# Sums of down-projection weights: eight of eleven moved from the in-projection to the out-projection, into slots of the raw weight ring

## The chip, the cores and the metric

The kernel runs on one core of a Trainium2 chip. The metric is the device time of one execution in microseconds (us). Engines are named as in the profile: PE is TensorE (PEld its weight loads), DVE is VectorE, ACT is ScalarE, POOL is GpSimd, SP is SyncE, whose instruction queue issues nearly all DMAs of this kernel. PE's order of instructions is written out by hand; the order on the other engines, and which buffer a tile gets, is decided by a scheduler when the program is built.

## The reference

One layer of a streaming encoder, in fp32. The input has 2048 prompt rows (16 tiles of 128) and one tile of 8 x 16 sample rows, of width 1024; the feed-forward part has width 2816.

```python
qm, km, vm, om, ip, fp, qa, ka, va = split_in(x @ w_in)
hm, C1, n1, m1 = mlstm_chunkwise(qm, km, vm, logi, logf, C0, n0, m0, mchunk)   # 4 heads x 128
hm = (og * head_norm(hm, g_mlstm_norm)).reshape(B, T, M_WIDTH)
ha = swa_prompt(rope(qa), rope(ka), va, attn_sinks)                            # 8 q, 2 kv heads x 64
mix = jnp.concatenate([hm, ha], axis=-1) @ w_out
h = layer_norm(DEEPNORM_ALPHA * x + mix, ln1_g, ln1_b)
f, conv_rows = conv_ffn(h, conv_prev, w_up, w_conv, b_conv, w_down)   # (silu(g) * a) @ w_down
y = layer_norm(DEEPNORM_ALPHA * h + f, ln2_g, ln2_b)
```

## The kernel before

Every product is made of three matmuls on halves: a fp32 operand is split into a high part (rounded, by ACT) and a low part (the rest, by DVE). Three of the four large projections also use a scheme with seven products of half-size blocks instead of eight, which needs sums and differences of blocks of the weights. The kernel runs in four stages: the in-projection (to about 625 us; four blocks of token tiles, `IBLOCKS`), the out-projection (about 626 to 905 us; five blocks `OBLOCKS` of 3, 4, 4, 4 and 2 tiles), the up-projection with convolution (to about 1840 us) and the down-projection. The mLSTM and attention work of each tile ("chains") is woven between the matmuls of the two projections before it is needed.

**The sums.** The down-projection needs differences of four quadrants of its weights: for each k from 0 to 10, rows of `wdn[k]` (x) and `wdn[11 + k]` (y). `d_sums` (L841) makes them ahead of time, in three steps that its caller gives out at chosen places: step 0 allocates the two tiles `txy` and issues the two loads of 512 KB on SP (L845, L846); step 1 makes four subtractions of 128 x 512 on DVE (L851 to L854), the first two on x's result and y, the others on both; step 2 stores both tiles to the DRAM arrays `zt[0, k]` and `zt[1, k]` (L856, L857). The arrays are read from 1838 us on (L2021). In the kernel before the tiles txy use the buffers `xr1` and `xr3` of the pool `xp`, which otherwise hold inputs: x of the in-projection and the pairs `xraw` of the out-projection (L893), each split into `oh` (ACT L897) and `ol` (DVE L898).

**The in-projection** (`i_dense`) walks over items (b, g, s): block b, weight group g of five, product s of seven. Before the change it gives out the steps of one sum in each of the items with b in (2, 3) and g in (0, 1, 2, 3): eight sums. Weights arrive in a ring of seven raw buffers, `wraw` (`WR = 7`, 4 KB in each partition): `next_raw` loads a unit into a slot, `next_split` splits it into `w` (ACT L218, DVE L219), after which the slot is free. `raw_free` allows at most four units (three once `spare` is set) to be loaded and not yet split, so that some slots of the ring stand idle.

**The out-projection** (`o_block`) makes each block in two halves of 512 output columns (`hf`). A half has eight matmul groups for each token tile; `group` yields after each of them, and `steps` counts them. A half takes four units of `wo` (L462), issued through the same ring. In the last round of half 1 the group loads the input pairs of the next block (`x_pair`). The result of a tile is taken out of PSUM by DVE into `ymix` (L1613), normalised later by `norm` (L1556 to L1573, with `lsc` on POOL, L1559), and stored to `zh`. Before the change three sums are given out here, in half 0 of blocks 1, 2 and 3.

**Queues.** A DMA in SP's queue waits for its data, for its buffer to be free, and for an earlier DMA that used the same semaphore; whatever stands behind it in the queue waits too. DVE and ACT also take their instructions in order. The steps of the chains that the prediction names: `dt`, `kw`, `qk` (L1110 to L1205) feed the matmul `pnum` (L1212); `mr` (L1154 to L1160), `ms` on POOL (L1161) and `hn` (L1157, L1167) feed the transposes `pht` (L1177); `ql` and `kringl` (L219) feed the scores `psc` (L1304), evicted by L1308; `pth` (L1344) feeds `ppo` (L1349). `cw` (L1674) is a scaling of the convolution's weights, at the end of the out-projection.

Of the kernel before, what the change touches and what calls it, by code (L numbers as in the profile page):

```python
# [8 lines left out]
F32 = mybir.dt.float32  # L9
# [5 lines left out]
P = 128  # L15
D = 1024
# [21 lines left out]
WR = 7  # L38
# [16 lines left out]
NK2 = NFF // 2  # L55
# [150 lines left out]
class Prog:  # L206
# [3 lines left out]
    def pool(self, name, bufs=1, space=None, **kw):  # L210
        if space is not None:
            kw["space"] = space
        return self.tc.tile_pool(name=name, bufs=bufs, **kw)
# [374 lines left out]
    def i_dense(self):  # L588
        nc, a = self.nc, self.a
        nb = len(IBLOCKS)  # L590
        last = NG - 1

        self.next_raw()
        self.x_load(0, 2)
        for _ in range(3):
            self.next_raw()
        self.x_load(0, 4)
        self.single_raw = self.tp.tile([P, KD, P], F32, name="xsr", tag="pth", bufs=2)
        nc.sync.dma_start(self.single_raw, a["xs"])
        self.angles = {}  # L600
        self.rope_load(IBLOCKS[0][2], 2)
        self.rope_load(NPT, 1)
        self.next_split()
        self.x_steps(0, "b12")
        for _ in range(3):
            self.next_split()
        self.x_steps(0, 3)
        self.x_single(1, 2)
        self.x_load(0, 1)
        self.next_raw()  # L610
        self.x_load(0, 3)
        self.x_steps(0, 1)
        self.advance()
        self.x_steps(0, 2, "t3", 7, "t2", 6)
        self.x_single(4)
        self.x_steps(0, "t1", 5, "t4")
        self.sb, self.trans = {}, None

        passages = [{1: ["load"], 7: ["t3", 7], 6: ["t2", 6], 3: [3, "t4"], 4: ["b12", "t1"]},
                    {1: ["load"], 6: ["t3"], 7: [7, "t2"], 5: [6], 3: [3, "t4"], 4: ["b12", "t1"]}]  # L620
        sums = 0
        after = None
        for item in self.items:
            if after:

                after[0] -= 1
                if after[0] == 3:
                    self.logs_of(after[1] - 1)
                if after[0] < 0:
                    self.i_done = after[1]  # L630
                    after = None
            self.chains.hold = item[0] == "t" and item[1] > 0
            if item[0] == "t":
                _, b, ti, e = item
                if ("g", e, 3) not in self.wu:
                    self.advance()
                if b not in self.gates:
                    self.gates[b] = self.tp.tile([P, 5, 8], F32, name="gates", tag="gates", bufs=2)
                ps = self.bank([P, 512], "pg") if ti == 4 else self.ib[ti % 2 * 2]
                yield from self.i_direct(b, ti, e, ps)  # L640
                self.i_keys(b, ti, ps)
                if ti == 1:
                    if b + 1 < nb:
                        self.x_steps(b + 1, 1, 2)
                    else:
                        self.release(4)
                    after = [6, b + 1]
                elif ti == 3 and b or ti == 4:
                    self.release(4)
                    self.x_steps(b, 4)  # L650
                    if b:
                        self.x_steps(b, 5)
                self.advance()
                continue
            _, b, g, s = item
            if item not in self.wu:
                self.advance()
            yield from self.i_product(b, g, s)
            del self.wu[item]
            self.release(2)  # L660
            if self.trans and s != 4:
                self.i_transposes()
            with self.tc.high_priority():
                behind = self.i_after(b, g, s)
            if (b, g, s) == (0, 0, 7):
                self.t_setup()
            if (g, s) == (1, 6):
                self.rope_load(IBLOCKS[b][0], 2)
            if g == last and b + 1 < nb:
                if s == 7:  # L670
                    self.rope_load(IBLOCKS[b + 1][2], 2)
                for x in passages[b > 0].get(s, ()):
                    if x == "load":
                        self.spare = True
                        self.x_load(b + 1, 1, 2, 3, 4)
                    else:
                        self.x_steps(b + 1, x)
            if g == last and b + 1 == nb and s in (7, 5, 2, 3):
                self.x_pair(0, (7, 5, 2, 3).index(s))
            with self.tc.issue_after(behind) if behind and b == 0 else nullcontext():  # L680
                self.advance()

            if b >= nb // 2 and g < last:

                steps = (6, 2, 5) if g == last - 1 else (6, 5, 3)
                if s in steps:
                    self.d_sums(sums, steps.index(s))
                    sums += s == steps[2]
        self.sums = sums
        self.logs_of(nb - 1)  # L690
        self.chains.hold = False
# [146 lines left out]
                              out[:, i * HT:(i + 1) * HT].rearrange("p (f m) -> p f m", f=2))  # L838


    def d_sums(self, k, step):  # L841
        nc, V = self.nc, self.nc.vector
        if step == 0:
            self.txy = x, y = [self.xp.tile([P, D], F32, name="txy", tag=f"xr{q}", bufs=1) for q in (1, 3)]
            nc.sync.dma_start(x, self.a["wdn"][k])  # L845
            nc.sync.dma_start(y, self.a["wdn"][NK2 + k])  # L846
            return
        x, y = self.txy
        if step == 1:
            l, r = slice(0, 512), slice(512, D)  # L850
            V.tensor_sub(x[:, l], x[:, r], x[:, l])  # L851
            V.tensor_sub(x[:, r], y[:, r], x[:, r])
            V.tensor_sub(y[:, r], y[:, r], x[:, l])
            V.tensor_sub(y[:, l], y[:, l], y[:, r])  # L854
            return
        nc.sync.dma_start(self.zt[0, k], x)  # L856
        nc.sync.dma_start(self.zt[1, k], y)  # L857
# [730 lines left out]
    def o_block(self, b):  # L1588
        nc, nb = self.nc, len(OBLOCKS)
        tiles = OBLOCKS[b]  # L1590

        ys = self.ynext + [self.o_x(t) for t in tiles[len(self.ynext):]]
        self.ynext = []

        outs = [self.fp.tile([P, D], F32, name="ymix", tag="hst", bufs=2) for _ in tiles] if b == nb - 1 else ys
        for hf in range(2):
            c = slice(hf * 512, hf * 512 + 512)
            steps = 0
            for cost, ti, ps in self.group(b, tiles, 8 * b + 4 * hf, hf == 1):
                yield cost  # L1600
                if ps is None:
                    steps += 1
                    if hf and b + 1 < nb and steps == 8 * len(tiles) - 6:
                        self.ynext = [self.o_x(t) for t in OBLOCKS[b + 1][:2]]
                    if steps % 2 == 0 and self.norms and next(self.norms[0], self) is self:
                        del self.norms[0]
                    if hf == 0 and b and self.sums < NK2 and steps in (2, 14, 20):
                        self.d_sums(self.sums, (2, 14, 20).index(steps))
                        self.sums += steps == 20
                    continue  # L1610
                y = outs[ti]
                with self.tc.high_priority():
                    nc.vector.scalar_tensor_tensor(y[:, c], ys[ti][:, c], ALPHA, ps, op0=ALU.mult, op1=ALU.add)  # L1613
                if hf and b == nb - 2 and ti >= len(tiles) - 2:

                    nc.sync.dma_start(self.zh[tiles[ti]], y)
                elif hf and b < nb - 1:
                    self.norms.append(self.norm(y, *self.ln1, self.zh[tiles[ti]]))
        assert b < nb - 1 or self.sums == NK2
        self.late = list(zip(outs, tiles))  # L1620
# [575 lines left out]
```

## Time and profile before

| | us |
|---|---|
| median of 3 runs | 2308.32 |
| lowest and highest | 2305.21, 2309.71 |
| profiled execution | 2306.25 |
| its span in the trace | 2304.5 |

The profile is of one execution. The span is the time from the first to the last instruction in it; the time of the execution is 1.75 us longer. A row of a timeline gives the start, the duration, the engine, the line, the operation with its tiles (out<-in) and, in brackets, the idle time of the engine before it and what ended it. A table of windows gives for each stretch the busy time of every engine. A view of waits sums up, for one engine, the idle time by the instruction that waited and by what it waited for.

### The profile page before, as it was taken

What the parts mean: (1) busy time and instruction counts of PE and PEld (TensorE: products, weight loads), DVE (VectorE), ACT (ScalarE), POOL (GpSimd) and SP (SyncE); (2) the same over time, 40 slices, a digit from 0 to 9 for tenths busy, and PEclk for the clock granted to TensorE, in tenths of its full rate; (3) what the DMA queues carried; (4) which work ended last, traced back from release to release, by engine and by line L of the source; (5) the groups of instructions that cost most, each with busy time, mean ns of one, the idle gap of its engine ahead of it and who ended that gap; (6) DMA issues with size and microseconds to landing.
All of it is one profiled execution on the core that took longest, in us unless ns stands there. A gap on an engine that the chain in (4) does not pass through costs nothing.

```text
span 2304.5 us, 39741 instructions
## 1 busy us (share of the span) xinstructions
PE 2278.9 (99%) x14293; PEld 2094.4 (91%) x14293; DVE 1807.4 (78%) x3075; ACT 1272.4 (55%) x2377; POOL 279.4 (12%) x509
## 2 busy tenths in 40 slices
PE   8999999999999999999999999999999999999998
PEld 8999999989877778999999999999999978888876
DVE  8787587787688888998778777678766786895987
ACT  5453476776766656555656555556555544444442
POOL 0001001100011210211112101003111200200200
PEclk9999999999999999999999999999999999999999
DMA  7988999899987757888777888878998786746742
GB/s 267 319 306 297 309 322 342 310 306 341 309 286 239 242 199 277 302 328 300 277 281 272 307 304 310 306 256 289 316 299 260 248 299 213 253 170 223 253 156 83
DMA packets 300165, 632.38 MB, mean 274 GB/s; under 512 B 47868, under 2 KB 141120, under 8 KB 299968
## 3 DMA queue, kind: packets, MB, share of 16 engines
q1 hardware_dynamic: 295296, 616.14, 77.3%
q0 software_dynamic: 3520, 10.56, 1.4%
q10 hardware_dynamic: 1152, 3.15, 0.4%
q8 instruction: 113, 1.85, 0.3%
q14 instruction: 84, 0.69, 0.1%
HBM read 458.11 MB, written 171.64 MB: 273 GB/s over the span
## 4 chain that ended last, share of the span: by engine, by line
PE 81%; DVE 4%; DMA 2%; issue 1%; ACT 1%; POOL 0%; SPq 0%; DVEq 0%; ACTq 0%; POOLq 0%
PE dps L1874 19%; PE fup L1874 19%; PE dps L705 8%; PE fup L2081 6%; PE dps L2081 6%; PE fht L2081 6%; PE dps L223 3%; PE dps L224 2%; PE dps L225 2%; PE ppo L1349 1%; PE psc L1304 1%; PE ppt L1343 1%; PE dps L731 1%; PE fht L1698 1%; PE pscore L1129 1%
## 5 line engine op out<-in xcount | busy, mean ns | idle before, releaser
L1874 PE MATMUL fup<-hh,uw 128*128 128x384 f32 (+1 forms) x1848 | 478.4, 328 | 0.0
L1874 PE MATMUL dps<-hh,uw 128*128 128x384 f32 (+1 forms) x1848 | 478.0, 328 | 0.0
L1874 PEld LDWEIGHTS fup<-hh,uw 128*128 128x128 f32 x1848 | 330.5, 188 | 0.0
L1874 PEld LDWEIGHTS dps<-hh,uw 128*128 128x128 f32 x1848 | 330.3, 188 | 0.0
L1932 DVE SCALAR_TENSOR_TENSOR cc<-u,cw,cc 128x768 f32<-128x768 f32 (+1 forms) x264 | 258.2, 979 | 62.8 <-ACT cc L1930 56.1
L1874 PE MATMUL fup<-hl,uw 128*128 128x384 f32 (+1 forms) x924 | 303.2, 328 | 0.9 <-DVE hl L219 0.9
L1874 PE MATMUL dps<-hl,uw 128*128 128x384 f32 (+1 forms) x924 | 302.8, 328 | 0.0
L705 PE MATMUL dps<-w,oh 128*128 128x256 f32 x1344 | 254.2, 284 | 0.0
L218 ACT CAST uw<-wraw 128x1024 fp32r<-128x1024 f32 x126 | 123.3, 979 | 230.4 <-PE dps L2081 122.4
L219 DVE TENSOR_TENSOR w<-wraw,w 128x1024 fp32r<-128x1024 f32 (+2 forms) x167 | 189.7, 1142 | 66.0 <-ACT w L218 61.9
L218 ACT CAST w<-wraw 128x1024 fp32r<-128x1024 f32 (+2 forms) x167 | 163.0, 984 | 119.0 <-PE dps L705 61.9
L705 PEld LDWEIGHTS dps<-w,oh 128*128 128x128 f32 x1344 | 210.7, 188 | 10.8 <-issue 8.1
L219 DVE TENSOR_TENSOR uw<-wraw,uw 128x1024 fp32r<-128x1024 f32 x126 | 142.5, 1131 | 62.3 <-ACT uw L218 62.2
L705 PE MATMUL dps<-w,ol 128*128 128x256 f32 x672 | 188.1, 280 | 0.0
L1874 PEld LDWEIGHTS fup<-hl,uw 128*128 128x128 f32 x924 | 173.9, 188 | 1.7 <-DVE hl L219 1.5
L2081 PE MATMUL fup<-uw,fu 128*128 128x512 f32 x726 | 174.0, 396 | 1.2 <-ACT fht L2089 1.2
L1874 PEld LDWEIGHTS dps<-hl,uw 128*128 128x128 f32 x924 | 173.8, 188 | 0.0
L705 PE MATMUL dps<-oh,w 128*128 128x256 f32 x896 | 169.6, 285 | 3.6 <-DVE w L219 1.3
L2081 PEld LDWEIGHTS fup<-uw,fu 128*128 128x128 f32 x726 | 136.6, 188 | 34.3 <-ACT fht L2089 1.6
L2081 PE MATMUL dps<-uw,fu 128*128 128x512 f32 x660 | 165.3, 396 | 1.1 <-DVE uw L219 1.1
L1930 ACT ACTIVATE cc<-u,cw 128x768 f32<-128x768 f32 (+1 forms) x132 | 132.0, 1001 | 46.2 <-DVE u L1912 22.2
L2081 PEld LDWEIGHTS dps<-uw,fu 128*128 128x128 f32 x660 | 124.1, 188 | 31.2 <-DVE uw L219 1.5
(318 smaller groups left out, 4590.0 us busy)
## 6 DMA issues: line engine op xcount, KB each, us to landing
uw<-zw SPq DMA_DIRECT2D x176, 512.0 KB, 5.1
zw<-uw SPq DMA_DIRECT2D x88, 512.0 KB, 3.3
w<-zws SPq DMA_DIRECT2D x72, 512.0 KB, 5.8
wv<-wup SPq DMA_DIRECT2D x66, 512.0 KB, 4.4
wraw<-wi SPq DMA_DIRECT2D x65, 512.0 KB, 5.5
wraw<-zt SPq DMA_DIRECT2D x60, 512.0 KB, 4.1
wraw<-wdn SPq DMA_DIRECT2D x45, 512.0 KB, 4.5
wraw<-wo SPq DMA_DIRECT2D x40, 512.0 KB, 4.7
```

The source lines that it names most:

```text
L218: nc.scalar.copy(hi, src)
L219: return nc.vector.tensor_sub(lo, src, hi.bitcast(F32)).ins
L223: mm(out, ah, bh, start=start, stop=False)
L224: mm(out, ah, bl, start=False, stop=False)
L225: mm(out, al, bh, start=False, stop=stop)
L705: mm(o, l, r, start=s in (1, 7) and c == k == i == 0, stop=k == 3 and i == 2, skip_group_check=True)
L731: mm(o, x, w, start=k == i == 0, stop=k == KD - 1 and i == 2, skip_group_check=True)
L1129: self.nc.tensor.matmul(ps[:, h], qk[:, 4 + h], qk[:, h], start=True, stop=True)
L1874: mm(ps, l[:, k], r[:, k], start=s in (1, 7) and k == 0 and i == 0, stop=k == 3 and i == 2, skip_group_check=True)
L1930: S.activation(c[:, v], u[:, 2:2 + n], AF.Identity, bias=w[3], scale=w[2])
L1932: V.scalar_tensor_tensor(c[:, v], u[:, i:i + n], w[i], c[:, v], op0=ALU.mult, op1=ALU.add)
L2081: mm(ps, l[:, k, c], r[:, k], start=s in (1, 4, 7) and u == 0 and k == 0 and i == 0, stop=u == nu - 1 and k == n - 1 and i == 2, skip_grou ...
```

## The change

Three sums stay in the in-projection, given out at (b, g) = (2, 1), (3, 0) and (3, 2). The other eight are given out in the out-projection, one in each half of blocks 0 to 3, at the steps 2 (loads), 18 (subtractions) and 22 (stores). Those eight take their two tiles from the ring of raw weights (`ring=True`) instead of `xr1` and `xr3`. The three that stay in the in-projection use `xr1` and `xr3` as before. The number of instructions, of DMAs and of bytes, and what they compute, stay the same, and so does the order of PE's instructions.

```diff
@@ i_dense
-            if b >= nb // 2 and g < last:
-
-                steps = (6, 2, 5) if g == last - 1 else (6, 5, 3)
+            if (b, g) in ((nb - 2, 1), (nb - 1, 0), (nb - 1, 2)):
+
+                steps = (6, 5, 3)
                 if s in steps:
                     self.d_sums(sums, steps.index(s))
                     sums += s == steps[2]
@@ d_sums
-    def d_sums(self, k, step):
+    def d_sums(self, k, step, ring=False):
         nc, V = self.nc, self.nc.vector
         if step == 0:
-            self.txy = x, y = [self.xp.tile([P, D], F32, name="txy", tag=f"xr{q}", bufs=1) for q in (1, 3)]
+            pool = lambda q: (self.wp, "wraw", WR) if ring else (self.xp, f"xr{q}", 1)
+            self.txy = x, y = [p.tile([P, D], F32, name="txy", tag=tag, bufs=n) for p, tag, n in (pool(1), pool(3))]
             nc.sync.dma_start(x, self.a["wdn"][k])
             nc.sync.dma_start(y, self.a["wdn"][NK2 + k])
             return
@@ o_block
-                    if hf == 0 and b and self.sums < NK2 and steps in (2, 14, 20):
-                        self.d_sums(self.sums, (2, 14, 20).index(steps))
-                        self.sums += steps == 20
+                    if self.sums < NK2 and steps in (2, 18, 22):
+                        self.d_sums(self.sums, (2, 18, 22).index(steps), True)
+                        self.sums += steps == 22
                     continue
```

## The prediction

> **What bounds the kernel now.** I read the totals of the page first, then a table by stage, then the waits of TensorE in the two stages that the change touches, then the rows around each sum.
>
> ```profile
> span 2304.5 us, 39741 instructions
> ...
> PE 2278.9 (99%) x14293; PEld 2094.4 (91%) x14293; DVE 1807.4 (78%) x3075; ACT 1272.4 (55%) x2377; POOL 279.4 (12%) x509
> ```
>
> TensorE (PE) is busy for 2278.9 us of 2304.5, so 25.6 us are idle in the whole kernel. The change touches no matmul. It can gain no more than the idle time that hangs on the moved sums, and it loses wherever a moved sum makes TensorE wait.
>
> The table by stage has, for each stretch, its length, then busy time of PE, PEld, DVE, ACT and POOL with instruction counts, the granted clock, the DMA share and GB/s.
>
> ```profile
> core 0: us, PE busy (x) PEld busy (x) DVE busy (x) ACT busy (x) POOL busy (x), PEclk, DMA share, GB/s
> ...
> 300.00:560.00 260.00, 255.83 (x2156) 237.01 (x2154) 200.26 (x573) 185.24 (x477) 25.75 (x43) 1.00 0.94 322
> ...
> 630.00:905.00 275.00, 274.86 (x1516) 216.60 (x1515) 229.99 (x552) 170.86 (x411) 42.91 (x51) 1.00 0.73 249
> ```
>
> The stretch 300 to 560 us holds the eight sums of the in-projection: DMA is nearly full (0.94), TensorE idles 260 - 255.83 = 4.17 us. The out-projection, 630 to 905, has room on the DMA engines (0.73), but TensorE idles 0.14 us: nothing can be won there. DVE has 275 - 229.99 = 45 us free. So the most that the change can bring is 4.17 us, 0.18% of the time. Which part of it hangs on sums is told by the waits of PE from 310 to 362 and from 480 to 560 (total us, times, longest):
>
> ```profile
> PE dps L705 <- ACT mr L1154: 0.8, 1, 0.8
> PE pht L1177 <- ACT hn L1167: 0.5, 1, 0.5
> PE pnum L1212 <- issue: 0.5, 1, 0.5
> ...
> PE pnum L1212 <- issue: 1.4, 1, 1.4
> PE ppo L1349 <- ACT pth L1344: 0.6, 1, 0.6
> PE pht L1177 <- DVE ql L219: 0.2, 1, 0.2
> ```
>
> Six waits, 4.0 us together. I number the sums 0 to 10 in order of time.
>
> **Part 1: five sums leave the in-projection.** A sum is two loads of 512 KB (x, y), four subtractions on DVE, two stores. The view of the tiles txy:
>
> ```profile
> L851 DVE TENSOR_TENSOR txy<-txy x11: 667/687/693, 311.0 to 827.2; 128x512 f32<-128x512 f32 x11
> ...
>   DVE txy L852: 4.6, 3
>   DVE txy L851: 3.8, 2
> ...
> DMA to landing us min/median/max: 3.1/4.9/8.2
> ```
>
> One subtraction takes 0.687 us, so a sum is 4 x 0.687 = 2.75 us of DVE, and the five take 13.7 us of DVE and 5 x 4 x 0.5 = 10.5 MB out of the stage. On DVE five waits for loads took 4.6 + 3.8 = 8.4 us. But three sums stay, and in the order built from the changed source they stand on each queue where sums 0, 4 and 5 stood; those that go are 1, 2, 3, 6 and 7. That matters, because the longest wait of PE belongs to sum 5:
>
> ```profile
> 495.52 0.69 DVE L851 TENSOR_TENSOR txy<-txy 128x512 f32<-128x512 f32 x1 [2.91 <-DMA txy<-wdn]
> ...
> 499.55 0.69 DVE L1133 TENSOR_TENSOR dt<-pscore,dt 128x512 f32<-128x512 f32 x1
> ...
> 500.34 0.46 PE L1212 MATMUL pnum<-v,dt 128*128 128x129 f32 x2 [1.43 <-issue]
> ```
>
> DVE waited 2.91 us for x; dt stood behind it; the matmul that reads dt started 0.1 us after dt's end (499.55 + 0.69) and PE had idled 1.43. The third kept sum has the same neighbours (amx, w, kw, dt), and its loads still follow at once on the two stores of the sum before, whose tiles they reuse. I take this wait as kept: 0, bounds 0 to 1.43. The 0.5 us before pnum and the 0.8 us on mr lie beside sum 0, which stays: 0, bounds 0 to 1.3. Two waits do hang on sums that go:
>
> ```profile
> 513.81 0.69 DVE L852 TENSOR_TENSOR txy<-txy 128x512 f32<-128x512 f32 x1 [3.55 <-DMA txy<-wdn]
> ...
> 515.89 0.66 PE L1177 MATMUL pht<-ident,hn 128*128 128x128 f32 x4 [0.20 <-DVE ql L219]
> ...
> 543.46 0.69 DVE L852 TENSOR_TENSOR txy<-txy 128x512 f32<-128x512 f32 x1
> 544.07 0.15 DVE L1159 SCALAR_TENSOR_TENSOR mr<-mr 128x4 f32<-128x4 f32 x1
> 544.19 0.69 DVE L853 TENSOR_TENSOR txy<-txy 128x512 f32<-128x512 f32 x1
> ...
> 546.55 1.28 ACT L1167 ACTIVATE hn<-hn,ms 128x128 f32<-128x128 f32 x4 [3.61 <-POOL ms L1161]
> ...
> 548.36 1.08 PE L1349 MATMUL ppo<-pth,kva 128*64 128x512 f32 x4 [0.64 <-ACT pth L1344]
> ```
>
> Sum 6 held ql for 3.55 us: 0.20 us of PE. Sum 7 put two subtractions (1.2 us, the gaps from 543.46 to 544.07 and 544.19 to 544.80) between the small steps of mr; ms on POOL and hn on ACT came as much later, pth queued behind hn, and PE lost 0.64, less than the 1.2 that goes. The last wait, 0.5 us for hn at 336, follows on an ms whose input was ready before sum 1's first subtraction: 0, bounds 0 to 0.5. So part 1 brings 0.64 + 0.20 = 0.84 us, bounds 0 and 4.05 (0.5 + 0.8 + 0.5 + 1.43 + 0.64 + 0.2, with the rounded rows).
>
> **Part 2: eight sums in the out-projection instead of three.** Five more are 13.7 us on DVE, which has 45 us free, and 10.5 MB more in 275 us, 38 GB/s on 249, where the stage before moved 322. On average both are covered; what counts is the place. The loads go into slots of the ring of raw weights, so x and y wait until a weight split has read its slot. For the sums of half 1 the second load goes out just ahead of its subtractions. Sum 4's place (block 0, half 1):
>
> ```profile
> 649.54 1.22 DVE L219 TENSOR_TENSOR w<-wraw,w 128x1024 fp32r<-128x1024 f32 x1
> ...
> 652.22 1.22 DVE L219 TENSOR_TENSOR w<-wraw,w 128x1024 fp32r<-128x1024 f32 x1
> ...
> 655.57 1.23 DVE L219 TENSOR_TENSOR w<-wraw,w 128x1024 fp32r<-128x1024 f32 x1 [0.23 <-ACT w L218]
> 658.11 0.20 DVE L1027 COPY col<-pcol 128x36 f32<-128x36 f32 x1 [1.32 <-PE pcol L1025]
> 661.02 0.42 DVE L1308 CUSTOM_DVE_ANT_0 sc<-psc,k_mswa 128x256 f32<-128x256 f32 x1 [2.71 <-PE psc L1304]
> ```
>
> x can go at 649.54 + 1.22 = 650.76, y at 652.22 + 1.22 = 653.44; with the median landing of 4.9 us they are there at 655.7 and 658.3. The sum follows the split that ends at 656.80, so DVE waits 658.3 - 656.8 less one subtraction (0.69) = 0.8 us and subtracts until 658.3 + 3 x 0.69 = 660.4. Queued behind are col (658.11) and the evictions of psc (661.02). Col is 2.3 us late; DVE itself idled 1.32 + 2.71 us at this place, so the evictions are on time. Sums 6 and 8 stand in like places; for sum 6:
>
> ```profile
> 707.33 2.37 DVE L219 TENSOR_TENSOR w<-wraw,w 128x1024 fp32r<-128x1024 f32 x2 [0.54 <-ACT w L218]
> ...
> 714.05 1.22 DVE L219 TENSOR_TENSOR w<-wraw,w 128x1024 fp32r<-128x1024 f32 x1
> ...
> 720.47 0.69 DVE L219 TENSOR_TENSOR ql<-pq,qh 128x512 fp32r<-128x512 f32 x1 [2.72 <-ACT qh L218]
> 721.28 0.68 DVE L1613 SCALAR_TENSOR_TENSOR ymix<-ymix,dps 128x512 f32<-128x512 f32 x1
> ```
>
> x goes at 709.7 and lands by 714.6, y at 715.3 and lands by 720.2. The first subtraction falls into the 2.72 us in which DVE waited for qh; ql keeps its time; the second one precedes the eviction of dps at 721.28, later by 0.7 us. TensorE waits for neither unless a bank runs out, which no row here shows. I take 0.3 us for each of the four half-1 sums, 1.2 us; bounds 0 and, at the longest landing (8.2, 3.3 more than the median, each passed on in full), 4 x 3.3 = 13.2.
>
> The next place is the start of a block, where the split of its last input pair was barely ahead of TensorE:
>
> ```profile
> 750.69 1.22 DVE L898 TENSOR_TENSOR ol<-xraw,oh 128x1024 fp32r<-128x1024 f32 x1
> ...
> 752.94 0.39 PE L225 MATMUL dps<-w,ol 128*128 128x512 f32 x1
> ```
>
> ol ended at 751.91, its first matmul ran at 752.94: 1.0 us of slack. A sum ahead of it in the queue would cost up to 2.75 - 1.0 = 1.7 us. In the changed order none stands directly ahead, and the idle DVE time before it (2.72 us at 720.47) covers sum 6: 0, bounds 0 to 1.7 at each of three such starts. At the start of block 4 the loads of its last pair and of cw go out later, behind weight loads that wait for a sum's store, but splits that stood behind the wait for cw now go first: 0, bounds -1 to 2.
>
> Stores: a weight load that takes a sum's slot over waits on SyncE's queue until the store has landed, and what is queued behind waits too. Loads of wo are issued tens of us ahead (DVE and ACT show no wait for one in this stage), so 0, bounds 0 to 2.
>
> A rule that speaks against the change concerns POOL, so first its rows: ms in all (min/median/max in ns), then the two that ran while a sum's subtractions ran on DVE.
>
> ```profile
> L1161 POOL TENSOR_TENSOR ms<-mr,mhalf x17: 1030/1865/2492, 225.4 to 849.0; 128x4 f32<-128x4 f32 x17
> ...
> 332.37 1.36 POOL L1161 TENSOR_TENSOR ms<-mr,mhalf 128x4 f32<-128x4 f32 x1 [9.60 <-DVE mr L1160]
> ...
> 545.11 1.41 POOL L1161 TENSOR_TENSOR ms<-mr,mhalf 128x4 f32<-128x4 f32 x1 [8.01 <-DVE mr L1160]
> ```
>
> The Trainium skill, "SBUF — State Buffer", section "Who interferes with whom", says that a DVE instruction with two SBUF inputs contends with a GpSimd instruction that reads SBUF. By it each moved sum could hold up an ms of the out-projection by a subtraction, and if four of them reached TensorE as at 548 the sum would grow by 4 x 0.69 = 2.8 us (an estimate). The trace does not bear it out: the two were shorter than the median, so the sum goes without it.
>
> **Sum**, against the profiled execution (2306.25 us, span 2304.5): -0.84 + 1.2 = +0.4, so 2306.6. The median of the runs shown is 2308.32, 2.1 above that execution, so 2308.7 in its terms.
>
> **The rivals.** *Late second load* (slower). The half-1 sums run in DVE's order ahead of chain work; should a y land late, everything behind it on DVE (col, psc and dps evictions, the next weight splits) shifts. It decides once landings of txy in this stage pass 6 us, the time from 715.3 to the eviction at 721.28. At 8.2 us for all four it costs 13.2: 2308.3 - 0.8 + 13.2 = 2320.7. For it: the same head-of-line waits in the in-projection took 8.4 us of DVE and one cost TensorE 1.43. Against it: the DMA share is 0.73 instead of 0.94, and DVE has gaps at three of the four places. *Whole relief* (faster): with 10.5 MB fewer, the loads of the kept sums come sooner and all six waits go, none arises: 2308.3 - 4.05 = 2304.3. Against it: sum 5's loads wait for stores of the sum before, which stays. *No effect*: the sums only trade hidden places, 2308.3.
>
> **How the numbers follow.** Forecast, no change that can be measured: 0.55, with no effect another 0.07; its own range is 2305.5 to 2313. Late second load, with the other bounds of part 2 beside it: 0.28. Whole relief: 0.10. A measurement of this kernel tells about 0.2% from no change, 4.6 us, so faster means below 2303.7 and slower above 2312.9. Whole relief lies at that edge and gives faster most of its chance, 0.07; late loads give slower 0.28 and the forecast's upper tail 0.03. The point is 2308.7. The range reaches down to 2303.5 (relief) and up to 2319 (most of the late loads).
>
> **What would show it.** Right: sum 5's wait near 495 and the 1.4 us before pnum are still there, the 0.6 us before ppo near 548 is gone; TensorE's idle time from 630 to 905 stays under 2 us; landings of txy there stay near 5 us. Wrong: waits of PE on evictions, ql or ol in the out-projection, each after a DVE wait for txy; TensorE idle there by 5 us or more; or no idle left from 300 to 560.

## The result, and the profile after

The changed kernel takes 2311.54 us (median of 21 runs, 2307.57 to 2316.10), the kernel before beside it 2307.47 us (21 runs). The ratio is 1.0015, 95% interval 1.0009 to 1.0021: 2 to 5 us slower. That lies within the 0.2% that the prediction took for no change, yet clear of zero: its point was 0.4 us above before.

The profiled execution took 2313.83 us, with a span of 2312.1. First its table by stage, in the columns of the same table before:

```profile
core 0: us, PE busy (x) PEld busy (x) DVE busy (x) ACT busy (x) POOL busy (x), PEclk, DMA share, GB/s
300.00:560.00 260.00, 257.76 (x2171) 239.07 (x2170) 191.91 (x560) 187.98 (x480) 21.78 (x43) 1.00 0.88 294
630.00:905.00 275.00, 270.10 (x1482) 211.25 (x1481) 233.85 (x554) 169.38 (x408) 43.27 (x48) 0.99 0.82 280
```

The in-projection idles 2.24 us on PE where it idled 4.17. The out-projection idles 4.90 where it idled 0.14. The DMA share moved as it had to, 0.94 to 0.88 and 0.73 to 0.82. The waits of PE from 560 to 910 us (total us, times, longest), of which there were none before:

```profile
PE fht L1699 <- DMA hst<-zh: 4.3, 3, 2.4
PE ppt L1344 <- ACT pth L1345: 0.3, 1, 0.3
```

So the loss is at one place: transposes `fht` for the up-projection, woven into the last block of the out-projection, wait for `hst`, rows of h (at 881, 883 and 887 us). The waits of DVE from 630 to 905 on sums and what stood behind them:

```profile
DVE txy L852 <- DMA txy<-wdn: 3.0, 2, 1.6
DVE txy L853 <- DMA txy<-wdn: 1.4, 1, 1.4
DVE w L219 <- DMA txy<-wdn: 1.4, 1, 1.4
```

DVE did wait 5.8 us at the moved sums, and no wait of PE is put down to a sum or to what stood behind one on DVE.

Why is hst late? SP's queue shows it, first before, then after (start, time in the issue, line, DMA; x4 are four issues in a row):

```profile
847.64 4.44 SPq L462 DMA_DIRECT2D wraw<-wo  x4
...
860.09 2.40 SPq L893 DMA_DIRECT2D xraw<-zmix  x3
...
863.13 0.43 SPq L893 DMA_DIRECT2D xraw<-zmix  x1
863.93 1.03 SPq L1672 DMA_DIRECT2D cw<-cw  x1
869.40 0.35 SPq L1585 DMA_DIRECT2D ymix<-x  x1
...
875.65 0.33 SPq L1771 DMA_DIRECT2D wv<-wup  x1
...
878.70 0.60 SPq L1773 DMA_DIRECT2D wg<-wup  x1
```

```profile
850.58 0.33 SPq L462 DMA_DIRECT2D wraw<-wo  x1
855.03 0.33 SPq L857 DMA_DIRECT2D zt<-txy  x1
856.48 0.33 SPq L858 DMA_DIRECT2D zt<-txy  x1
...
857.71 0.55 SPq L462 DMA_DIRECT2D wraw<-wo  x1
...
860.48 0.37 SPq L894 DMA_DIRECT2D xraw<-zmix  x1
...
862.02 0.44 SPq L894 DMA_DIRECT2D xraw<-zmix  x1
862.50 0.87 SPq L462 DMA_DIRECT2D wraw<-wo  x1
865.82 0.34 SPq L1586 DMA_DIRECT2D ymix<-x  x1
866.21 3.10 SPq L894 DMA_DIRECT2D xraw<-zmix  x2
869.68 0.34 SPq L1673 DMA_DIRECT2D cw<-cw  x1
...
871.17 0.33 SPq L1772 DMA_DIRECT2D wv<-wup  x1
872.19 0.41 SPq L1774 DMA_DIRECT2D wg<-wup  x1
```

Before, the last four weight loads of wo are out by 852 us, and the four input pairs of the last block by 863.5. After, the last sum (k = 10) holds two slots of the ring until its stores at 855.0 and 856.5; two weight loads go out only at 857.7 and 862.5, ahead of the first pair and among the pairs, and the last pair goes out at about 869 instead of 863. What the queue waited for from 856 to 870 us, after the change:

```profile
SPq L1586 <- DMA zh<-ymix: 2.4, 1, 2.4
SPq L894 <- DMA hst<-zh: 2.3, 1, 2.3
...
SPq L462 <- DMA zt<-txy: 0.3, 1, 0.3
```

The weight loads themselves waited only 0.3 us for the sum's stores. The pairs are late through the order that the queue now has: the load `ymix<-x`, which before stood behind all four pairs, now stands ahead of the last two and waits 2.4 us for a store of h, and the last pair waits 2.3 us for an earlier load of hst. ACT, which issues the loads of hst, stands behind the pairs: the first of the last four goes out at 873.46, with the `oh` that had waited 3.5 us for its pair. ACT's waits from 855 to 892, before and after:

```profile
ACT oh L897 <- DMA xraw<-zmix: 3.4, 1, 3.4
```

```profile
ACT oh L898 <- DMA xraw<-zmix: 10.8, 3, 5.1
```

The hst loads before and after, as ACT issued them:

```profile
867.91 0.33 ACTq L1716 DMA_DIRECT2D hst<-zh  x1
871.53 0.33 ACTq L1714 DMA_DIRECT2D hst<-zh  x1
873.01 0.33 ACTq L1714 DMA_DIRECT2D hst<-zh  x1
875.29 0.33 ACTq L1716 DMA_DIRECT2D hst<-zh  x1
```

```profile
873.46 0.33 ACTq L1717 DMA_DIRECT2D hst<-zh  x1
874.29 0.81 ACTq L1715 DMA_DIRECT2D hst<-zh  x2
875.76 0.34 ACTq L1717 DMA_DIRECT2D hst<-zh  x1
```

Four loads that were spread over 7.4 us go out within 2.3. Before, all four were out ahead of `wv` and `wg`, the first weight loads of the up-projection (512 KB each); now those two go out first. The trace gives the landing of the first and the third of the four: before after 6.1 and 3.6 us, now after 7.8 and 10.3. So the first is late mostly by its issue (5.6 of 7.3 us), the third mostly by its landing (6.7 of 8.4). PE's table in steps of 2 us shows the end of it:

```profile
884.00:886.00 2.00, 0.57 (x3) 0.13 (x1) 0.69 (x1) 0.49 (x1) 0.00 (x0) 1.00 1.01 414
886.00:888.00 2.00, 0.99 (x5) 1.02 (x6) 0.00 (x0) 0.00 (x0) 0.00 (x0) 0.74 0.94 385
888.00:890.00 2.00, 2.00 (x8) 1.63 (x7) 1.25 (x1) 1.17 (x2) 0.00 (x0) 0.50 0.04 16
890.00:892.00 2.00, 2.00 (x13) 1.76 (x12) 1.11 (x2) 1.05 (x2) 0.00 (x0) 0.90 0.00 0
```

On top of the wait, the granted clock falls to 0.74, 0.50 and 0.90 of full speed: up to 2 x (0.26 + 0.50 + 0.10) = 1.7 us more (PE was busy for only part of the first 2 us).

### The profile page after: what moved, and what is told of

The parts are those of the page before. It is cut to its first block, busy times and chain, and to the rows that moved or that the text cites. A ratio compares the mean times of both kernels' runs of the same rounds, so it can differ in the third digit from the quotient of the medians.

```text
span 2312.1 us, 39744 instructions
## 1 busy us (share of the span) xinstructions
PE 2282.0 (99%) x14293; PEld 2094.2 (91%) x14293; DVE 1807.7 (78%) x3075; ACT 1272.9 (55%) x2377; POOL 271.3 (12%) x509
## 4 chain that ended last, share of the span: by engine, by line
PE 79%; DVE 5%; DMA 3%; issue 1%; ACT 1%; SPq 0%; POOL 0%; DVEq 0%; ACTq 0%; POOLq 0%
PE fup L1875 18%; PE dps L1875 18%; PE dps L705 9%; PE fup L2082 6%; PE dps L2082 6%; PE fht L2082 6%; PE dps L223 2%; PE dps L224 2%; PE dps L225 2%; PE ppo L1350 1%; PE ppt L1344 1%; PE psc L1305 1%; DMA zf<-cc 1%; DVE cc L1933 1%; PE dps L731 1%
```

## The experiments

Three theories. A: the last sum alone costs, by crowding the queue and the DMA engines ahead of hst. B: the other sums of the out-projection, or the ring as such, cost as well. C: the difference arises in later stages.

**A fourth sum in the in-projection, none in block 3's half 1.**

```diff
-            if (b, g) in ((nb - 2, 1), (nb - 1, 0), (nb - 1, 2)):
+            if (b, g) in ((nb - 2, 1), (nb - 2, 3), (nb - 1, 0), (nb - 1, 2)):
```

> The changed kernel with a fourth sum in the in-projection, at (2, 3), so that block 3's half 1 of the out-projection has none. Theory A (the last sum crowds the DMA engines and SyncE's queue just ahead of the first loads of h for the up-projection, so the transposes wait): the waits of PE on hst (4.3 us in three in the changed kernel) are gone, PE idles under 1 us from 630 to 910, the time is 3 to 5 us below the changed kernel and 0 to 3 us below the kernel before. Theory B (the sums of the other halves, or the ring, cost time as well): still 2 us or more above the kernel before. Theory C (the difference of the two kernels lies in later stages, not in the sums): hst waits gone, time as the changed kernel, ratio to before 1.001 to 1.002.

2305.31 us against 2306.11, ratio 0.9991 (0.9982 to 1.0000). PE waits on hst no more; from 630 to 910 it idles 1.92 us (1.4 of it for pth), more than the 1 us that A allowed. A fits, B and C do not.

**Without the last sum.**

```diff
-                    if self.sums < NK2 and steps in (2, 18, 22):
+                    if self.sums < NK2 - 1 and steps in (2, 18, 22):
...
```

> The changed kernel without the last sum (k = 10: no loads, subtractions or stores; the down-projection reads the rows of k = 9 in its place). Theory A: as with the fourth sum in the in-projection, PE's waits on hst gone, ratio to before 0.998 to 1.0005. Theory B: PE still waits in the out-projection for 2 us or more. Theory C: ratio 1.001 to 1.002.

Ratio 0.9996 (0.9987 to 1.0005), no hst wait, PE idle from 630 to 910 is 1.23 us (4.90 in the changed kernel).

**The last sum made but not stored.**

```diff
+        if k == NK2 - 1:
+            return
         nc.sync.dma_start(self.zt[0, k], x)
         nc.sync.dma_start(self.zt[1, k], y)
...
```

> The changed kernel with the last sum loaded and subtracted but not stored (the down-projection reads the rows of k = 9 in its place). If the stores and the weight loads that wait for them make the crowd: the hst waits fall from 4.3 us to under 1. If the sum's loads, or its place on DVE, are enough: they stay at 3 us or more. Half of both: 1 to 3 us.

Ratio 1.0006 (0.9997 to 1.0016). The hst waits are gone, but others come: PE waits 1.0 us for ol, 0.7 for dt, 0.4 for a split, and idles 2.98 us from 630 to 910. Without the store the last weight loads go out by 857 and the pairs by 865.5, still later than the 863.5 before. The stores make the worst of the hst waits; the time of this run is not told apart from that of either kernel.

**The in-projection's part alone.**

```diff
-                    if self.sums < NK2 and steps in (2, 18, 22):
+                    if False:
...
```

> Only the three sums of the in-projection are made, at the changed kernel's places; the eight sums of the out-projection are left out (the down-projection reads rows of k = 0 to 2 in their place). It shows what the five sums less in the in-projection bring, free of the out-projection. By the changed kernel's trace: PE idles about 2.2 us from 300 to 560 (4.2 in the kernel before), nothing from 630 to 910, so 2 us below the kernel before, ratio 0.999. By the prediction's sum: 0.8 us below (sum 5's wait stays), ratio 0.9996. If the relief of DMA matters further on: 4 us or more below, ratio 0.998.

2304.20 us against 2306.11, ratio 0.9989 (0.9980 to 0.9998); PE idles 1.79 us from 300 to 560 (and 1.13 from 630 to 910, where nothing was expected). The five sums less bring about 2.5 us (0.5 to 4.6), not 0.8. This run also lacks the three sums that the kernel before makes in the out-projection, but there PE had idled only 0.14 us.

**The changed kernel again.** Its code is the changed kernel's, without any edit.

> The changed kernel once more, unchanged, beside the following runs. If the waits of its first profile belong to the program: PE waits on hst again for 3 to 5 us in the out-projection, and on ua for about 1.2 us near 1648, ratio to before 1.001 to 1.002. If either is chance of one execution, it is missing or under half.

Ratio 1.0010 (1.0000 to 1.0020). The hst waits are there again, 4.1 us in two. The wait on ua near 1648 (1.2 us in the first profile) is 0.4 here: chance, for its larger part.

**The out-projection's part alone.**

```diff
-            if (b, g) in ((nb - 2, 1), (nb - 1, 0), (nb - 1, 2)):
-                steps = (6, 5, 3)
+            if b >= nb // 2 and g < last:
+                steps = (6, 2, 5) if g == last - 1 else (6, 5, 3)
...
-        self.sums = sums
+        self.sums = 3
```

> The part of the change in the out-projection alone: the in-projection as in the kernel before with its eight sums, and the out-projection as in the changed kernel with eight sums (k = 3 to 7 are made a second time). Theory A (the out-projection costs about 5 us, the in-projection brings about 2): the sum of the parts, ratio to before 1.002 (4 to 6 us slower), hst waits of 3 to 5 us, and PE idle from 300 to 560 as before, 4 us with sum 5's 1.4 us. Theory B (the out-projection costs 3 and the in-projection nothing): ratio 1.001 to 1.0015.

Ratio 1.0027 (1.0016 to 1.0038), 6.2 us; hst waits of 3.4 us, PE idle from 300 to 560 of 4.23. The parts add up: +6.2 - 2.5 = +3.7 us, and the whole change is 1.0015, 3.5 us; the intervals of the parts are 4 to 5 us wide, so this agreement says little. Sum 5's 1.4 us, expected here, was not there.

**The last sum in xr1 and xr3.** Same bytes, same work, but no weight load takes over its slots.

```diff
-                        self.d_sums(self.sums, (2, 18, 22).index(steps), True)
+                        self.d_sums(self.sums, (2, 18, 22).index(steps), self.sums < NK2 - 1)
```

> The changed kernel with the last sum's two tiles in xr1 and xr3 instead of the ring, so that no weight load of the last block waits for its stores; bytes and work are the same. If the order in SyncE's queue (weight loads behind the stores) makes the hst wait: it falls under 1 us, ratio 0.9995 to 1.0005. If the bytes alone do: it stays at 3 us or more, ratio as the changed kernel's. A new wait may arise, as two pairs xraw of the last block wait for the same two buffers.

2305.18 us against 2307.91, ratio 0.9984 (0.9975 to 0.9993): faster than expected and than the kernel before. The changed kernel beside it took 2310.70, so these two slots cost about 5.5 us. Its waits of PE from 560 to 910:

```profile
PE pnum L1213 <- DVE dt L1134: 1.3, 1, 1.3
PE fup L1875 <- DVE hl L219: 0.3, 1, 0.3
PE ppt L1344 <- ACT pth L1345: 0.3, 1, 0.3
```

Nothing waits for hst. But this run changes two things: xr1 and xr3 are free earlier than the ring's slots, so the sum's stores too come earlier (840 and 844 instead of 855 and 856.5). The last run tells these apart.

**Another place for the fourth sum.**

```diff
-            if (b, g) in ((nb - 2, 1), (nb - 1, 0), (nb - 1, 2)):
+            if (b, g) in ((nb - 2, 0), (nb - 2, 2), (nb - 1, 0), (nb - 1, 2)):
```

> Four sums in the in-projection, at (2, 0), (2, 2), (3, 0), (3, 2), and seven in the out-projection, none in block 3's half 1: another place for the sum that the first such kernel put at (2, 3). By theory A no hst wait, ratio 0.998 to 0.9995. If the place of the fourth sum in the in-projection matters (PE idled 0.65 us more there with (2, 3)): PE idle from 300 to 560 is under 2.5 us instead of 2.9.

2304.57 us against 2307.91, ratio 0.9981 (0.9971 to 0.9991). PE idles 1.92 us from 300 to 560 and 0.92 from 630 to 910. Like the kernel with the last sum in xr1 and xr3, this version beats both kernels; the two are not to be told apart.

**The kernel before again.** Without any edit.

> The kernel before once more, unchanged, for a second profile of it. If the wait at sum 5 (DVE 2.9 us for the load, PE 1.4 us before pnum) belongs to the program, it is there again at 1 us or more of PE; if it was chance of one execution (with the in-projection unchanged and the out-projection of the changed kernel it was not there), it is missing, and the idle time from 300 to 560 is spread otherwise. Ratio 1.000.

Ratio 1.0007 (0.9998 to 1.0016). Its waits of PE from 300 to 560:

```profile
PE ppo L1350 <- ACT pth L1345: 1.6, 1, 1.6
PE pht L1178 <- DVE ql L219: 1.5, 1, 1.5
...
PE pnum L1213 <- issue: 0.5, 1, 0.5
```

Sum 5's wait is missing (DVE waited 0.62 us for x): it was chance of the first profile. The waits at sums 6 and 7, for ql and for pth, are there, and larger: 3.1 us instead of 0.84. PE idles 5.39 us in the stage.

**All eight sums in xr1 and xr3.**

```diff
-                        self.d_sums(self.sums, (2, 18, 22).index(steps), True)
+                        self.d_sums(self.sums, (2, 18, 22).index(steps))
```

> The changed kernel with all eight sums of the out-projection in xr1 and xr3 instead of the ring. Pairs xraw of the next block then wait for a sum's stores, and the sums for the splits of the pairs. If only the last sum's ring slot costs: as with the last sum alone in xr1 and xr3, ratio 0.998 to 0.999. If the ring is what keeps the other seven out of the way: PE waits for ol or oh at the starts of blocks, 3 us or more from 630 to 910, ratio 1.000 or more.

Ratio 1.0006 (0.9997 to 1.0015), between the two expectations. PE idles 2.73 us from 630 to 910, 1.5 of it at ppt and 0.8 at pgr, none of it for ol or oh and none for hst. The queue of SP in this run decides what the run before left open:

```profile
849.06 4.93 SPq L462 DMA_DIRECT2D wraw<-wo  x4
854.26 0.33 SPq L857 DMA_DIRECT2D zt<-txy  x1
855.71 0.33 SPq L858 DMA_DIRECT2D zt<-txy  x1
...
862.54 1.78 SPq L894 DMA_DIRECT2D xraw<-zmix  x3
```

The last sum's stores go out at 854.3 and 855.7, as late as in the changed kernel, with the same bytes. But the four weight loads are ahead of them, all four pairs are ahead of `ymix<-x` again, and the last two 256 KB loads of hst land after 4.4 and 3.9 us. So neither the late stores nor the bytes make hst wait: what is left is the order of the queue that the ring slot brings, with two weight loads behind the stores. The time of this run does not show the gain of the kernel with the last sum alone in xr1 and xr3. It has the waits named above, and its granted clock fell to 0.74, 0.50 and 0.90 from 682 to 688 us, behind the 1.5 us at ppt.

## Why the prediction was right or wrong

The time fell in the range, and the end, slower by less than 0.2%, was among its cases. That was in part luck: against the sum's -0.84 and +1.2 us the two parts alone measured about -2.5 and +6.2, and the errors, of opposite sign, cancelled in part. Of the signs that the prediction named, two failed: PE's idle time from 630 to 905 was 4.90 us, not under 2, and sum 5's wait was gone.

**Right: which stage wins, which loses, and what can be won.** PE idled 4.17 and 5.39 us from 300 to 560 in two profiles of the kernel before, 2.24 and 1.93 in two of the changed one. Of the six waits, those at sums 6 and 7 went, and those at 310 to 362 stayed.

**Mis-sized: the gain of part 1.** The step said 0.64 + 0.20 = 0.84 us. The part alone brought about 2.5 us. The mechanism, ql and mr held up by the sums that go, was right; the price came from one profile in which these two waits were small (3.1 us in the second). (The upper bound of 4.05 adds up to 4.07.) Sum 5's 1.43 us went as well, but the second profile of before, with sum 5 unchanged, did not have it either: it is no gain of the change.

**Mis-sized: the half-1 sums.** The step priced late second loads at 4 x 0.3 = 1.2 us. DVE waited 5.8 us at sums of the out-projection, and PE waited for none of it: 0. The rival of the late second load, at 13.2 us, did not happen, although some landings of txy in the stage passed its 6 us (median 4.9, longest 6.8); no profile shows PE waiting on psc, col or dps evictions behind a sum.

**Failed: "Stores: ... Loads of wo are issued tens of us ahead, ... so 0, bounds 0 to 2", with the start of block 4 at "0, bounds -1 to 2".** Here the change loses: hst waits of 4.3, 4.1 and 3.4 us in the three profiles with the last sum made in the ring and stored, none in the seven other variants, nor in the two profiles of the kernel before. The mechanism was named, that a weight load waits on the queue until a store has landed and what is queued behind waits too. For the sums before the last, 0 was right: over the whole stage loads of wo waited 20.1 us on SP's queue for sums' stores (12 times), and PE waited for none. What the step missed is who is queued beside the last two weight loads: those two waited only 0.3 us for the stores, but the last two pairs of block 4 came behind them and behind `ymix<-x`, and the pairs gate ACT, which issues hst; no step of the prediction looked at hst at all. Both bounds were too tight by about 2 us.

The part alone cost 6.2 us by its ratio, of which the hst waits are 3.4 and the lower clock behind them (next section but one) up to 1.7; the rest is within the interval's width.

**The contention on POOL** did not show: the median of the seven ms from 630 to 905 is 1.96 us with the eight sums after 1.89 with three, and PE's waits from 560 to 910 are for hst, but for 0.3 us for pth.

**Left open.** Why the late hst loads land so slowly is not shown. In all three profiles with hst waits `wv` and `wg` are both issued ahead of the last four loads of hst, in the nine others never both; that fits the two being in the way, but no run moves them alone. The wait on ua in the up-projection varied from 0 to 2.3 us over the profiles without an order that the sums explain.

## What to carry to other kernels

When a tile is given an idle slot of a ring, look at the next tenant of that slot: its load can be issued only behind the guest's store, and the order of the whole queue may change with it. The slack of the next tenant itself is not enough; read the new order up to the last loads before a stage change, which here is where the slack ended, and leave that one slot alone. A wait that is read from one profile may be chance: two profiles of the kernel before put 1.4 us in different places.

## What the runs showed of the hardware

TensorE's granted clock fell to half behind the hst waits, in two of three profiles: in the changed kernel to 0.74, 0.50 and 0.90 from 886 to 892 us, after 2.44 us of waiting, and with the out-projection's part alone to 0.95, 0.50 and 0.70 from 888 to 894. In the second profile of the changed kernel the clock stayed at 1.00 at this place, though its longest wait, 3.1 us, was longer than the other two's.

Such drops are not tied to hst. Behind other waits the clock fell from 682 to 688 us with all eight sums in xr1 and xr3 (after 1.5 us), from 548 to 552 with the out-projection's part alone (after 1.75), from 250 to 256 and from 1858 to 1864 in the second profile of the kernel before, and from 1860 to 1864 in that of the changed one. The length of a wait does not decide it: the 2.9 us wait for `v` near 250 us stands in all twelve profiles, and the clock fell behind it in one. Counted as above, each of these drops is worth 1.7 us, which is 3.4 us at half the clock.

The Trainium skill, "TensorE: Matmul & The Clock Gate", section "What's actually happening", describes a free-running window of about 3.4 us of activity by which the clock is cut to half and released. A window that runs free fits both that the drop lasted about that long and that the longest wait had none; no run here shows the window itself. The section puts the cut after at least one idle window; here the clock fell behind single waits of 1.5 to 2.9 us, shorter than that, and not behind each of them.
